# Sums of squares of queries and keys: one fp32 product or two fp32r products of split squares

## The chip, the cores and the metric

The kernel runs on one core of one Trainium2 chip. The metric is the device time of one execution in microseconds (us), the median of several runs. A core has TensorE (PE, which multiplies matrices, its weight loads are written PEld), VectorE (DVE), ScalarE (ACT), GpSimd (POOL), and SyncE (SP), whose queue issues most of the DMAs.

## What is computed

One step of a two-layer streaming encoder for 1024 frames of a new stream and 32 frames of a running one, 1056 tokens in all, model width 1024. Layer 0 mixes tokens by forgetting attention with 16 heads of 64 features, layer 1 by a gated linear recurrence; each is followed by a squared-ReLU MLP. The change touches the norms of queries and keys in layer 0, one norm for each token and head:

```python
def rmsnorm(x, g):
    xf = x.astype(jnp.float32)
    y = xf * lax.rsqrt(jnp.mean(xf * xf, axis=-1, keepdims=True) + EPS)
    return (y * g.astype(jnp.float32)).astype(x.dtype)

def fox_mixer(h, w_in, b_f, g_q, g_k, w_out, past_k, past_v, past_logf):
    proj = h @ w_in
    q = proj[..., :D_MODEL].reshape(B, T, FOX_HEADS, FOX_HEAD_DIM)
    k = proj[..., D_MODEL:2 * D_MODEL].reshape(B, T, FOX_HEADS, FOX_HEAD_DIM)
    ...
    q = rmsnorm(q, g_q)
    k = rmsnorm(k, g_k)
```

## The kernel before

Everything is fp32 in and out. The large products run in fp32r, a form of fp32 with fewer bits: each operand is split into a high part (the value rounded to fp32r) and a low part (what is left), and a product is three fp32r products (`mm3`, L152 to L158, all recorded at L158). A weight is split in `load_w` (L122 to L146): rounded on ScalarE or GpSimd, subtracted on VectorE.

The 1056 tokens are three chunks of 352 columns (`C`), with features on the 128 partitions. In `fox`, pairs of heads (128 features) are taken one after the other. For a pair, `fox_pair` makes the projections v, k and q, three chunks each, 24 products a chunk (`proj`, tile `pj`); `fox_attend` then does the attention of the pair in two halves: first the row maxima of the logits (`mp`, reduced on VectorE), then, block by block, logits (`st`), their exponentials on ScalarE (`pf`), the split of these on GpSimd (`ph`, after a causal mask on the diagonal blocks) and VectorE (`pl`), and the products with the values (`pv`). The next pair's projections run beside the attention of the pair before: v and k mostly beside the maxima, q beside the second half.

Each chunk of k and of q goes through `ev_norm` (L745 to L757). ScalarE copies the product out of PSUM (`raw`, L750) and squares it (`sq`, L751). TensorE sums the squares over the 64 features of each head, and spreads the sum over these 64 partitions, by a product with `blk`, a matrix of two blocks of ones (`ss`, L753, fp32). `rsqrt` (L197 to L210) takes that to the power -1/2: a logarithm and an exponential on ScalarE (L203, L206), a Newton step of three instructions on VectorE (L208 to L210, with a scratch tile of tag `nt`). L756 multiplies. There are 8 pairs x 2 x 3 = 48 such chunks.

Buffers on this path: `pj` and `ss` share two PSUM buffers (tag A), `raw` and `sq` have two buffers each, `nt` and `qr` one each. Raw weights have two buffers (tag `wr`).

`late_consts` (L94 to L97) loads `blk` and the causal mask `tri` with one DMA while the first chunk is normed. It is called behind the first weight loads.

The order of instructions on each engine is not the order of the text. The framework plans it when the kernel is built, by the priority of an instruction (its place in the text, unless raised) and by when its inputs and a buffer for its output are expected to be ready. At run time each engine goes through its own list in order and waits on semaphores.

Of the kernel before, what the change touches and what calls it, by code (L numbers as in the profile page):

```python
# [7 lines left out]
F32 = mybir.dt.float32  # L8
F32R = mybir.dt.float32r
# [24 lines left out]
def consts():  # L34
# [11 lines left out]
    # pairs of key s and query t: in one block of four, then in the two halves of larger blocks  # L46
# [13 lines left out]
class K:  # L60
# [21 lines left out]
    def gains(self):  # L82
        # gains, features of a tile on partitions: loaded in rows, turned on the tensor engine
# [9 lines left out]
    # constants that the first products do not need  # L93
    def late_consts(self):  # L94
        m = self.cp.tile([128, 2, 128], F32, name="mats")
        self.nc.sync.dma_start(m, self.io["c_mats"][:, 1:3])
        self.blk, self.tri = m[:, 0], m[:, 1]  # L97
# [7 lines left out]
    # what frees PSUM goes ahead of other work  # L105
# [3 lines left out]
    # an order of two instructions on one engine  # L109
# [11 lines left out]
    # one unit of weights: [128, X, Y] with X*Y = 1024, split exactly into two float32r parts  # L121
# [29 lines left out]
    # out += W^T x over the given k tiles; each product in three float32r passes  # L151
# [12 lines left out]
    # per token of a chunk, tokens on partitions in three columns (the last one overlaps the  # L164
    # second): sums over all features of s, [128, C]
# [8 lines left out]
    # such columns as rows along the free axis, the same on every partition  # L174
# [7 lines left out]
    # running sum over feature tiles of y ** 2: [128, C], features of a tile on partitions  # L182
# [13 lines left out]
    # r = (ss / n + eps) ** -0.5  # L196
    def rsqrt(self, r, ss, n, pool):  # L197
# [9 lines left out]
        # one Newton step  # L207
# [13 lines left out]
    # x * gain in split form; y is scratch  # L221
# [13 lines left out]
    # the norm's factor per token, which the products take on later: as columns, or as rows  # L235
    def prestat(self, x, y, rows):
# [13 lines left out]
        # the product's factor is the square, which the norm after it takes to the square again  # L250
# [4 lines left out]
    # the norm's factor per token of y * sc, for y; ss the sums of y ** 2  # L255
# [14 lines left out]
    # x += rmsnorm(y * sc), sc a factor per token, acc the sum of y ** 2; y is overwritten  # L270
# [52 lines left out]
    # the last chunk of the output is normed with tokens on partitions, in three blocks (the last  # L323
    # one overlaps the second). Ahead of that: x in that form, and the gains on diagonals
# [43 lines left out]
    # one token chunk of the input: loaded with tokens on partitions,  # L368
# [11 lines left out]
    # brought to features on partitions, with the first norm's factor per token,  # L380
# [37 lines left out]
    # normed and split  # L418
# [14 lines left out]
    # mixer's output (features on partitions, split, per token chunk) -> W_out -> norms ->  # L433
    # squared-ReLU MLP -> norms; returns the next layer's h, or writes the outputs
    def tail(self, os, w_out, layer, rs=None, after=None):
# [5 lines left out]
        with ExitStack() as c:  # L441
# [10 lines left out]
            # output projection  # L452
# [3 lines left out]
            # a factor of the norm before the products is less urgent than the next chunk's norms  # L456
# [24 lines left out]
            # MLP, G tiles of the hidden layer at a time  # L481
# [27 lines left out]
            # one output tile of the second matrix, over the given hidden tiles  # L509
# [27 lines left out]
            # the first three tiles of the hidden layer token chunk by token chunk, as the norms finish  # L537
# [12 lines left out]
            for g in range(NG - 2):  # L550
# [8 lines left out]
                for o in range(NJ):  # L559
                    for n in range(NCH):  # L560
                        down_one(g == 0, us, dw, o, n)
                us = nxt
            # the last two groups token chunk by token chunk, so that the norms overlap the products;
            # the last group's second weights in an h tile that is free by then
            dw = down_w(NG - 2)
            w = up_w(NG - 1)
            nxt = [u_tile() for i in range(G)]
# [751 lines left out]
```

## Time and profile before

| what | value |
|---|---|
| time, median of 3 runs | 2999.41 us (2998.34 to 3000.39) |
| span of the profiled execution | 2996.0 us |
| TensorE busy | 2942.2 us, 98% |
| VectorE busy | 1734.0 us, 58% |
| ScalarE busy | 934.1 us, 31% |
| GpSimd busy | 967.0 us, 32% |

The profile is one execution of the program. Its span lies 3.4 us under the median of the runs. PE's busy time includes the time in which one matmul fills the array while the one before drains, so a busy PE is not one at its peak. Register, semaphore and DMA-issuing instructions are not counted as busy. The forgetting attention's part lies in the first 700 us.

### The profile page before, as it was taken

To read this page: it belongs to the slowest core of one execution; us is meant where nothing else is said; L and a number is where in the kernel's file an instruction comes from. 1 tells how busy PE (TensorE), PEld (TensorE's weight loads), DVE (VectorE), ACT (ScalarE), POOL (GpSimd) and SP (SyncE) were. 2 spreads that over 40 slices of the span, in tenths; PEclk is the share of its full clock that TensorE was granted. 3 is DMA by queue.
4 is the path that set the end of the run, shared out by engine and by line. 5 is a ranking of instruction groups with operands and counts; after the bars stand their busy time and mean duration, and the time that the engine had idled before them with its cause. 6 is when DMAs were issued, how large, how long until landed. Compare 5 with 4: busy or idle time off the path is not lost.

```text
span 2996.0 us, 46448 instructions
## 1 busy us (share of the span) xinstructions
PE 2942.2 (98%) x18511; PEld 2855.2 (95%) x18511; DVE 1734.0 (58%) x2980; ACT 934.1 (31%) x1915; POOL 967.0 (32%) x1151
## 2 busy tenths in 40 slices
PE   7999999999999999999998999999999999999999
PEld 6888888899999999999997999999999999999998
DVE  6788888874544444445468656654474454454545
ACT  5455555555432111111133122212353111111112
POOL 3345444531432112121145444433362121121223
PEclk9999999999999999999999999999999999999999
DMA  5221121134321111121122111104432111111112
GB/s 152 62 52 44 48 53 48 51 112 147 106 74 57 43 43 50 36 57 49 37 82 95 35 59 41 47 27 120 140 118 76 36 57 43 43 50 36 57 61 69
DMA packets 217817, 195.59 MB, mean 65 GB/s; under 512 B 14312, under 2 KB 193648, under 8 KB 217472
## 3 DMA queue, kind: packets, MB, share of 16 engines
q1 hardware_dynamic: 216576, 192.49, 21.5%
q8 instruction: 145, 2.38, 0.3%
q14 instruction: 72, 0.59, 0.1%
q0 software_dynamic: 1024, 0.13, 0.0%
HBM read 147.00 MB, written 45.52 MB: 64 GB/s over the span
## 4 chain that ended last, share of the span: by engine, by line
PE 89%; DVE 5%; issue 1%; POOL 1%; ACT 1%; DMA 1%; SPq 0%; DVEq 0%; POOLq 0%; ACTq 0%
PE up L158 24%; PE dn L158 24%; PE hj L158 8%; PE pj L158 8%; PE gp L158 6%; PE po L158 5%; PE lv L1166 1%; PE ss L753 1%; PE pv L880 1%; PE pv L879 1%; PE pv L878 1%; PE st L867 1%; PE st L866 1%; PE mp L835 1%; PE lv L1181 1%
## 5 line engine op out<-in xcount | busy, mean ns | idle before, releaser
L520 DVE TENSOR_TENSOR ya<-dn,ya 128x352 f32<-128x352 f32 x672 | 348.3, 522 | 550.4 <-PE dn L158 550.4
L162 POOL TENSOR_TENSOR rl<-rl 128x352 f32<-128x352 f32 x192 | 190.2, 999 | 1031.7 <-ACT uh L501 1029.3
L145 DVE TENSOR_TENSOR wl<-wr,wh 128x1024 fp32r<-128x1024 f32 x203 | 280.4, 1382 | 147.0 <-ACT wh L142 84.6
L158 PE MATMUL dn<-uh,wl 128*128 128x352 f32 x1440 | 356.9, 323 | 0.0
L158 PE MATMUL dn<-uh,wh 128*128 128x352 f32 x1440 | 353.7, 324 | 2.5 <-DVE ya L520 2.5
L158 PE MATMUL dn<-ul,wh 128*128 128x352 f32 x1440 | 353.5, 323 | 0.0
L499 ACT ACTIVATE rl<-up 128x352 f32<-128x352 f32 x192 | 88.8, 463 | 783.1 <-PE up L158 712.8
L158 PE MATMUL up<-hh,wl 128*128 128x352 f32 x1536 | 291.5, 323 | 0.0
L158 PE MATMUL up<-hh,wh 128*128 128x352 f32 x1536 | 287.5, 323 | 2.1 <-ACT wh L142 1.7
L158 PE MATMUL up<-hl,wh 128*128 128x352 f32 x1536 | 288.1, 323 | 0.0
L158 PEld LDWEIGHTS up<-hh,wh 128*128 128x128 f32 x1536 | 253.5, 188 | 3.1 <-ACT wh L142 2.3
L158 PEld LDWEIGHTS dn<-uh,wh 128*128 128x128 f32 x1440 | 251.3, 188 | 4.4 <-DVE ya L520 4.4
L158 PEld LDWEIGHTS up<-hh,wl 128*128 128x128 f32 x1536 | 254.4, 188 | 0.0
L158 PEld LDWEIGHTS up<-hl,wh 128*128 128x128 f32 x1536 | 254.1, 188 | 0.0
L158 PEld LDWEIGHTS dn<-uh,wl 128*128 128x128 f32 x1440 | 252.6, 188 | 0.0
L158 PEld LDWEIGHTS dn<-ul,wh 128*128 128x128 f32 x1440 | 251.8, 188 | 0.0
L144 POOL TENSOR_SCALAR wh<-wr 128x1024 fp32r<-128x1024 f32 x109 | 120.8, 1108 | 294.3 <-PE pj L158 93.0
L503 DVE TENSOR_TENSOR ul<-rl,uh 128x352 fp32r<-128x352 f32 x192 | 142.6, 754 | 124.9 <-POOL rl L162 124.8
L142 ACT CAST wh<-wr 128x1024 fp32r<-128x1024 f32 x94 | 98.7, 1050 | 347.2 <-PE up L158 221.5
L876 DVE TENSOR_TENSOR pl<-pf,ph 128x512 fp32r<-128x512 f32 x192 | 124.5, 652 | 59.9 <-POOL ph L875 34.7
L875 POOL TENSOR_SCALAR ph<-pf 128x512 fp32r<-128x512 f32 x192 | 125.2, 654 | 51.6 <-PE pv L879 24.7
L869 ACT ACTIVATE pf<-st,ncol 128x512 f32<-128x512 f32 x192 | 109.7, 578 | 71.2 <-PE st L867 40.1
(343 smaller groups left out, 5673.0 us busy)
## 6 DMA issues: line engine op xcount, KB each, us to landing
wr<-in_ffn_w_up_dram SPq DMA_DIRECT2D x64, 512.0 KB, 4.0
wr<-in_ffn_w_down_dram SPq DMA_DIRECT2D x64, 512.0 KB, 3.8
wr<-in_fox_w_in_dram SPq DMA_DIRECT2D x32, 512.0 KB, 4.1
wr<-in_hgrn_w_in_dram SPq DMA_DIRECT2D x32, 512.0 KB, 4.1
x<-xd SPq DMA_DIRECT2D x22, 704.0 KB, 4.9
xd<-x SPq DMA_DIRECT2D x18, 704.0 KB, 3.1
out_dram<-tk SPq DMA_DIRECT2D x32, 256.0 KB, 2.4
odg<-go SPq DMA_DIRECT2D x30, 176.0 KB, 2.5
```

The lines of the kernel that those rows point to most:

```text
L142: self.s.copy(wh, raw)
L144: self.g.tensor_scalar(out=wh, in0=raw, scalar1=1.0, scalar2=0.0, op0=ALU.mult, op1=ALU.add)
L145: self.v.tensor_tensor(wl, raw, wh.bitcast(F32), op=ALU.subtract)
L158: self.nc.tensor.matmul(ps, lhsT=ws[kk][a], rhs=xs[kk][b], start=i == 0, stop=i == tot - 1)
L162: self.g.tensor_tensor(out, a, b, op=op)
L499: self.s.activation(rl, ps[:, :C], AF.Relu)
L503: self.v.tensor_tensor(ul, rl, uh.bitcast(F32), op=ALU.subtract)
L520: self.v.tensor_tensor(ys[n][:, o], ps[:, :C], ys[n][:, o], op=ALU.add)
L753: nc.tensor.matmul(ss[:, :C], lhsT=self.blk, rhs=sq, start=True, stop=True)
L869: self.s.activation(pf[:, :N], ps[:, :N], AF.Exp, bias=self.ncol[:, b, head:head + 1])
L875: self.g.tensor_scalar(out=ph[:, :N], in0=pf[:, :N], scalar1=1.0, scalar2=0.0, op0=ALU.mult, op1=ALU.add)
L876: self.v.tensor_tensor(pl[:, :N], pf[:, :N], ph[:, :N].bitcast(F32), op=ALU.subtract)
```

## The change

The square of a chunk is split in two fp32r parts, as weights are: ScalarE rounds it (`sh`), GpSimd subtracts (`sl_`), and the fp32 product with `blk` becomes two fp32r products that add up in PSUM. `sh` takes the second buffer of tag `sq`, `sl_` the single buffer of tag `nt`. `blk` is made fp32r by a copy on VectorE, from a raw tile of tag `wr`; its load and that of `tri` are two DMAs. Comments are removed all over the file, so most line numbers stay. The lines that count:

```diff
     def late_consts(self):
-        m = self.cp.tile([128, 2, 128], F32, name="mats")
-        self.nc.sync.dma_start(m, self.io["c_mats"][:, 1:3])
-        self.blk, self.tri = m[:, 0], m[:, 1]
+        self.tri = self.cp.tile([128, 128], F32, name="tri")
+        self.nc.sync.dma_start(self.tri, self.io["c_mats"][:, 2])
+        m = self.wp.tile([128, 128], F32, name="bl", tag="wr", bufs=2)
+        self.nc.sync.dma_start(m, self.io["c_mats"][:, 1])
+        self.blk = self.cp.tile([128, 128], F32R, name="blk")
+        self.v.tensor_copy(self.blk, m)
...
                 self.s.copy(raw, ps)
                 self.s.activation(sq, ps, AF.Square)
+                sh = pool.tile([128, C], F32R, name=f"sh{u}", tag="sq", bufs=2)
+                sl_ = pool.tile([128, C], F32R, name=f"sl{u}", tag="nt", bufs=1)
+                self.s.copy(sh, sq)
+                self.gtt(sl_, sq, sh.bitcast(F32), ALU.subtract)
                 ss = psp.tile([128, 512], F32, name=f"ss{u}", tag="A", bufs=2)
-                nc.tensor.matmul(ss[:, :C], lhsT=self.blk, rhs=sq, start=True, stop=True)
+                nc.tensor.matmul(ss[:, :C], lhsT=self.blk, rhs=sh, start=True, stop=False)
+                nc.tensor.matmul(ss[:, :C], lhsT=self.blk, rhs=sl_, start=False, stop=True)
```

## Rows read from the trace of the kernel before

**Rows 1.** The page: span, busy time and share of each engine, instructions.

```profile
span 2996.0 us, 46448 instructions
...
PE 2942.2 (98%) x18511; PEld 2855.2 (95%) x18511; DVE 1734.0 (58%) x2980; ACT 934.1 (31%) x1915; POOL 967.0 (32%) x1151
```

**Rows 2.** The page: the chain that ended last, by engine.

```profile
PE 89%; DVE 5%; issue 1%; POOL 1%; ACT 1%; DMA 1%; SPq 0%; DVEq 0%; POOLq 0%; ACTq 0%
```

**Rows 3.** Table by stage: length, busy us (instructions) of each engine, clock, DMA.

```profile
80.00:90.00 10.00, 7.34 (x38) 6.04 (x37) 9.81 (x15) 4.95 (x9) 4.66 (x5) 0.83 0.31 81
90.00:100.00 10.00, 9.06 (x55) 8.05 (x54) 6.91 (x15) 4.96 (x11) 1.03 (x1) 1.00 0.20 56
...
130.00:590.00 460.00, 454.65 (x2594) 409.04 (x2594) 382.94 (x810) 249.34 (x500) 221.03 (x369) 1.00 0.19 48
```

**Rows 4.** Groups to 1100 us: out<-in, shape, count | busy us, mean ns | idle before.

```profile
L158 PE MATMUL pj<-hl,wh 128*128 128x352 f32 x576 | 127.2, 327 | 0.0
...
L753 PE MATMUL ss<-sq,mats 128*128 128x352 f32 x96 | 39.9, 498 | 7.2 <-ACT sq L751 7.1
...
L426 ACT CAST hh<-y 128x352 fp32r<-128x352 f32 x24 | 11.5, 485 | 13.2 <-DVE y L424 13.0
```

**Rows 5.** Timeline beside the attention's second half: start us, us, instruction, count [wait].

```profile
136.73 0.76 PE L753 MATMUL ss<-sq,mats 128*128 128x352 f32 x2
137.06 1.72 PE L158 MATMUL pj<-hh,wh 128*128 128x352 f32 x8
138.62 1.45 PE L158 MATMUL pj<-hh,wl 128*128 128x352 f32 x8
...
157.27 0.47 ACT L751 ACTIVATE sq<-pj 128x352 f32<-128x352 f32 x1
...
159.72 0.75 PE L753 MATMUL ss<-sq,mats 128*128 128x352 f32 x2
```

**Rows 6.** Tile hl to 130 us: count, ns min/median/max, first and last start.

```profile
L430 DVE TENSOR_TENSOR hl<-y,hh x18: 509/517/2675, 19.7 to 66.4; 128x352 fp32r<-128x352 f32 x18
L162 POOL TENSOR_TENSOR hl<-y,hh x6: 942/1068/1205, 19.2 to 62.2; 128x352 fp32r<-128x352 f32 x6
```

**Rows 7.** Timeline beside the maxima, a chunk of k of pair 1.

```profile
121.83 0.79 PE L835 MATMUL mp<-KB,QX 96*128 96x512 f32 x3
...
122.35 0.47 ACT L751 ACTIVATE sq<-pj 128x352 f32<-128x352 f32 x1
...
122.87 0.86 PE L753 MATMUL ss<-sq,mats 128*128 128x352 f32 x2 [0.26 <-ACT sq L751]
...
123.30 1.72 PE L158 MATMUL pj<-hh,wh 128*128 128x352 f32 x8
...
124.89 0.53 DVE L208 SCALAR_TENSOR_TENSOR nt<-ss,qr 128x352 f32<-128x352 f32 x1 [0.74 <-ACT qr L206]
```

**Rows 8.** Timeline of pair 0, first chunk of q.

```profile
84.66 1.54 PE L753 MATMUL ss<-sq,mats 128*128 128x352 f32 x2 [1.31 <-ACT sq L751]
...
85.48 2.78 PE L158 MATMUL pj<-hh,wh 128*128 128x352 f32 x8
```

**Rows 9.** Waits to 620 us: who <- whom, us in total, times, longest.

```profile
PE ss L753 <- ACT sq L751: 7.1, 21, 1.3
...
PE pv L878 <- POOL ph L875: 1.3, 4, 0.3
```

**Rows 10.** Timeline of SP's queue and of GpSimd at the start.

```profile
11.57 0.42 SPq L132 DMA_DIRECT2D wr<-in_fox_w_in_dram  x1
12.05 0.57 SPq L96 DMA_DIRECT2D mats<-in_c_mats_dram  x1
...
17.86 2.26 SPq L631 DMA_DIRECT2D xd<-x  x4
...
21.52 2.50 POOL L139 TENSOR_TENSOR wl<-wr,wh 128x1024 fp32r<-128x1024 f32 x1
```

**Rows 11.** Tile ss, product with blk: records, ns min/median/max, first and last start.

```profile
L753 PE MATMUL ss<-sq,mats x96: 457/459/956, 39.7 to 587.0; 128*128 128x352 f32 x96
```

## The prediction

> **What bounds the kernel now.** I read the page first: TensorE is busy for 98% of the span, no other engine for more than 58% [rows 1], and the chain that ended last lies on PE for 89% of it [rows 2]. So time on PE is time of the kernel, unless PE is waiting. The change touches only the forgetting attention, so the second view is the table of stages. From 130 to 590 us, where pairs 1 to 7 are projected beside the attention of the pair ahead, PE is busy for 454.65 of 460 us at the full granted clock (1.00, that is 2.4 GHz); VectorE for 383, ScalarE for 249, GpSimd for 221 [rows 3]. Ahead of that, with pair 0 alone, PE has 0.9 to 2.7 us of idle time in ten, and in one stretch the granted clock is 0.83 [rows 3].
>
> Third view: the groups. The product with blk runs 48 times (8 pairs, q and k, 3 chunks) and shows as 96 records, two for each fp32 product [rows 4]. What one holds of PE is read from its neighbours: `ss` starts at 136.73, the eight `pj` behind it take 1.72 us where the next eight take 1.45 [rows 5], so the first of them was held back by 0.27 us and starts in effect at 137.32. One `ss` holds PE for 0.59 us. Eight `pj` of fp32r in 1.45 us, one of them lasting 0.33 (the mean of `pj`), are (1.45 - 0.33)/7 = 0.16 us each [rows 4, 5].
>
> **The change, part by part.** *The product in two passes.* Two fp32r products of the same 352 columns take 2 x 0.16 = 0.33 us in place of 0.59: 0.26 us less on PE for each, 48 x 0.26 = 12.5 us in all. In the saturated stretch and just ahead of it lie the 42 of pairs 1 to 7: 42 x 0.26 = 11. The six of pair 0 lie where PE waits anyway; I count nothing for them.
>
> The Trainium skill (Trainium Kernel Development and Optimization, Performance Expectations) holds matmul busy time a bad measure, because matmuls are pipelined, and takes the busy share of LDWEIGHTS. Here the two differ, 454.65 against 409.04 us of 460 [rows 3]; by that rule only 89% of the stretch is filled, and the 11 us would be 9.8.
>
> *Removed wait, added wait.* Today `ss` needs the square. From now on it needs the square, a copy of it to fp32r on ScalarE and the subtraction on GpSimd. The copy: 0.49 us, as the cast of a tile of this size from SBUF [rows 4]. The subtraction: 1.07 us, between 0.94 and 1.21, as the one `hl` of this shape on GpSimd [rows 6]. Hop between engines 0.05 us (square ends at 122.82, `ss` starts at 122.87 [rows 7]). So the sums start 1.65 us later; the product itself ends 0.49 us after its start and no longer 0.76 [rows 5], so the factor is 1.4 us later.
>
> Who waits for that? Queued behind `ss` on PE is the next chunk of the projection, 24 products or 3.9 us. It shares two PSUM buffers with `ss`: one is held by the chunk just done until its square is read, the other goes to `ss`. In 46 of the 48 the next product of a projection or gate stands directly behind `ss` (three of them are in [rows 5, 7, 8]; behind the first two come the forget gates'); both come free with the square. With the change the chunk is ready 1.6 us before `ss`, and since the order on each engine is planned ahead by readiness and priority, I take it that the 24 products go first and `ss` falls among them. Then the chunk covers the new wait. Beside the attention's second half there is more cover: at 157.27 the square begins, `ss` stands at 159.72 only, because attention's products rank ahead [rows 5]: the 1.6 us fit into that 2 us.
>
> What does not fit: in the first half (the maxima, `mp`), three short products fill the gap, then PE waits 0.26 us for the square [rows 7]; 21 such waits are 7.1 us in all [rows 9]. If `pj` takes the place of `ss` there, it waits for the same square, so that stays; if the free buffer lets it start at once, the waits vanish. Bounds: 0 to -7 us; I take 0, nearest to the rows.
>
> Lateness: PE goes in its fixed order, so a subtraction that comes later than planned holds up everything behind `ss`. The nearest row is the attention's own chain over the same engines, `st`, ScalarE, GpSimd, `pv`: in 192 of them PE waits four times, 1.3 us in all, 0.3 at most [rows 9]. Bounds: 0 to 48 x 0.3 = 14 us; I take 1, by that row.
>
> *Load on the other engines.* ScalarE gets 48 x 0.49 = 24 us, GpSimd 48 x 1.07 = 51 us; in the stretch they go from 54% to 59% and from 48% to 58%, no bound. VectorE gains no instruction but company: the same subtraction on VectorE ranges from 0.51 to 2.68 us in the first 130 us [rows 6], and I put the spread down to GpSimd's work beside it. If each of the 42 costs VectorE between 0 and 1.07 us, that is up to 45 of its 77 idle us; PE waits for it rarely. I take 1 us.
>
> *Buffers.* sh is the second `sq` buffer, free once the `ss` before it is done. sl is the one `nt` buffer, which the Newton step of the chunk before holds. That loop: subtraction 1.07, from `ss` to the first Newton step 2.0 us (122.87 to 124.89), three steps of 0.53 [rows 7]: 4.7 us against 3.9 + 0.33 = 4.2 us of PE per chunk when nothing lies between, as in pair 0, and about 6 beside `mp`. So at most 0.5 us for a few chunks of pair 0. There the chain from the square to the next chunk is on the path (1.31 us of wait at 84.66, and the next eight `pj` take 2.78 us, at about half the clock, after that idle time [rows 8]); bounds for the four late chunks: 4 x 1.4 = +5.6 if nothing covers, -2 if the wait goes. I take +1.
>
> *Constants.* One DMA of two matrices becomes two, and blk's half goes through a weight buffer (`wr`) and a copy on VectorE. On SP's queue it stands behind the weight load at 11.57; waiting for a buffer, it can hold back the stores of x and the small loads behind it until GpSimd has split those weights, at 24.0 [rows 10]. blk is first used at 39.7 [rows 11]. The copy is under the 0.51 us of a tile 2.75 times as wide. Cover 15 us: nothing; were it gone, the loads of the third chunk's x would come later, some 3 us.
>
> **The sum.** -11 + 0 + 1 + 1 + 1 = -8, rounded outward a little for the waits that may go: -9. The profiled span is 2996.0 us [rows 1], so 2987 by the profile; the median of the runs is 3.4 us above that span, which the change leaves as it is: 2990.4, say 2990. About 0.2% (6 us) is what a measurement of this kernel can tell from no change; 9 us is 0.3%.
>
> **The rivals.**
> *More than the passes.* The next `pj` uses the free PSUM buffer at once, and PE no longer empties at each `ss` beside `mp` and in pair 0: 7 us of waits [rows 9] and some of the emptied pipeline go too. 2990 - 11 = 2979. For it: PE did nothing else in the gaps; against: in today's order no `pj` stands ahead of the `ss` before it.
> *Given back.* `ss` is planned too early, the subtraction stands in GpSimd's queue behind ph, or ph behind it, and PE waits 0.26 us each: the gain of the passes is gone, 2999. For it: PE already waits 7.1/21 = 0.34 us at an `ss` for a chain of two steps that was planned to be ready [rows 9]; against: `pv` [rows 9].
> *PE waits out the subtraction.* If the next `pj` may not take its PSUM buffer before `ss` has one, PE has nothing but `mp` in the new 1.4 us. Place: the 21 `ss` of k in pairs 1 to 7 and six of pair 0. Price 27 x 1.4 - 12.5 = +25 us, 3024. It decides from the point where the mean new wait at an `ss` is above 0.26 us. For it: `ss` ahead of `pj` without exception; against: both come free with the same square, which explains that too. The Trainium skill (GPSIMD Engine Reference, 4.1 Engine selection) speaks against the place of the subtraction: it puts a two-input elementwise operation on GpSimd at about twice VectorE's time and sends it to VectorE; the trace agrees, 1068 against 517 ns [rows 6], and what hangs on it is the longest link of the new wait.
> *The passes are no shorter.* If fp32r products on blk took as long as the halves of the fp32 one, 0.3 us, nothing is gained: 3001. Against it speak all `pj`.
>
> **How the numbers follow.** Forecast 0.50, more than the passes 0.12, given back 0.18, waits out 0.17, no shorter 0.03. The forecast's own range, 2985 to 2997, has some 0.04 of its 0.50 within 0.2%; given back has 0.03 of its 0.18 beyond 0.2% on the slow side. Faster 0.46 + 0.12 = 0.58; same 0.04 + 0.15 + 0.03 (no shorter) = 0.22; slower 0.17 + 0.03 = 0.20. The range goes from 2976 to 3012: the low end takes in the first rival and its bound, the high end the bound of lateness (14 us) and half of the way into the third rival; what is left out is under 0.2.
>
> **What would show it.** `ss` as 96 fp32r records of about 0.32 us, 0.33 us from the first to the next `pj`; `ss` standing among `pj` of the next chunk; the group of waits of PE at `ss` for GpSimd small (under 3 us); the stage from 130 to about 590 shorter by 8 to 11 us, and everything behind it unchanged but earlier. Wrong would be: PE waiting for `sl` at most `ss`, `pj` still directly behind `ss`, or longer waits at `pv` for ph.

## The result, and the profile of the changed kernel

The changed kernel takes 3041.9 us in the median (3038.6 to 3042.9), the kernel before 2999.4: 42.5 us or 1.4% slower, ratio 1.0137 [1.0125, 1.0149]. The forecast was 2990, and its range ended at 3012.

Where the time went is read in three steps. First the page of the changed kernel: its span is 45.2 us longer, and the busy time of TensorE (PE) has not become less, as the shorter passes would have it, but 13.5 us more than in [rows 1].

```profile
span 3041.2 us, 46598 instructions
...
PE 2955.7 (97%) x18511; PEld 2867.5 (94%) x18511; DVE 1751.6 (58%) x2981; ACT 946.9 (31%) x1963; POOL 1036.1 (34%) x1199
```

Second, a landmark behind the change: the first product of the MLP, `up`. It starts at 817.9 us in the kernel before and at 861.6 in the changed one; the last starts at 2938.7 and 2984.0. So 43.7 of the 45 us are lost ahead of the MLP, in the forgetting attention. (Columns: instructions, ns min/median/max, first and last start. Kernel before, then the changed kernel.)

```profile
L158 PE MATMUL up<-hh,wh x1536: 317/323/430, 817.9 to 2938.7; 128*128 128x352 f32 x192
```

```profile
L161 PE MATMUL up<-hh,wh x1536: 317/323/427, 861.6 to 2984.0; 128*128 128x352 f32 x192
```

Third, the table by stage (columns as in [rows 3]). The first `ss` of pair 1 starts at 116.8 us in the kernel before and at 130.0 in the changed one, so nearly equal work lies from 30 to those points (458 and 446 of PE's records), and from there to the first `up`. The kernel before:

```profile
30.00:116.80 86.80, 77.51 (x458) 69.93 (x456) 61.86 (x130) 43.41 (x101) 23.64 (x23) 0.98 0.35 99
116.80:817.90 701.10, 692.64 (x4037) 638.41 (x4038) 534.01 (x1094) 372.56 (x748) 305.61 (x487) 1.00 0.26 72
```

The changed kernel, with the stretch of [rows 3] beside it:

```profile
30.00:130.00 100.00, 80.36 (x446) 73.29 (x444) 61.87 (x126) 44.58 (x104) 31.64 (x29) 0.91 0.30 87
130.00:861.60 731.60, 700.91 (x4040) 645.42 (x4040) 551.58 (x1100) 382.74 (x789) 368.41 (x529) 0.98 0.24 69
...
130.00:590.00 460.00, 434.35 (x2444) 389.82 (x2444) 374.27 (x783) 239.21 (x500) 255.59 (x371) 0.98 0.17 45
```

Pair 0 costs 13.2 us more (100.0 against 86.8), the rest of the attention 30.5 (731.6 against 701.1). PE's idle time (length less busy time) grows from 9.3 to 19.6 us in the first part and from 8.5 to 30.7 in the second, 32.6 us together. Its busy time grows by 2.9 and 8.3 us. The passes took 12.5 us off it, so some 24 us of busy time are work at a lower clock: the granted clock is 0.91 and 0.98 in place of 0.98 and 1.00 (an estimate from these rows). From 130 to 590 us PE idles 25.7 us, against 5.4 in [rows 3].

The passes are as short as forecast: 0.33 us each where [rows 11] had two records of 0.46.

```profile
L761 PE MATMUL ss<-sh,blk x48: 318/326/662, 37.8 to 637.0; 128*128 128x352 f32 x48
...
L762 PE MATMUL ss<-sl,blk x48: 318/327/432, 38.6 to 641.3; 128*128 128x352 f32 x48
```

The waits of PE up to 620 us, to be held against [rows 9]. The subtraction (L165, sl) is near the end of the list, 0.9 us in all. In front stand other works of ScalarE and VectorE, none of which the change touches: tk, pl, the casts hh, the maxima mx. Beside them PE waits 2.2 us, in three, for a Newton step (nt) that had yet to read `ss` and so to free its PSUM buffer.

```profile
PE to L776 <- ACT tk L778: 8.8, 7, 2.7
PE pv L889 <- DVE pl L885: 6.7, 10, 1.4
PE fz L161 <- ACT hh L429: 6.6, 7, 3.1
PE st L875 <- DVE mx L852: 5.0, 4, 1.3
...
PE ss L762 <- POOL sl L165: 0.9, 2, 0.6
```

What has happened is in the timeline of a chunk of k, pair 1, beside the maxima as in [rows 7] (start us, us, instruction, [idle before it <- releaser]). TensorE:

```profile
130.00 0.42 PE L761 MATMUL ss<-sh,blk 128*128 128x352 f32 x1
130.25 1.46 PE L161 MATMUL pj<-hh,wh 128*128 128x352 f32 x8
...
134.12 0.32 PE L762 MATMUL ss<-sl,blk 128*128 128x352 f32 x1
...
136.71 0.43 PE L761 MATMUL ss<-sh,blk 128*128 128x352 f32 x1
...
142.03 0.33 PE L762 MATMUL ss<-sl,blk 128*128 128x352 f32 x1
...
145.75 0.47 PE L875 MATMUL st<-QA,KA 128*128 128x512 f32 x1 [1.26 <-DVE mx L852]
...
146.72 2.58 PE L161 MATMUL pj<-hh,wh 128*128 128x352 f32 x8
```

GpSimd and ScalarE in the same stretch:

```profile
130.01 0.96 POOL L165 TENSOR_TENSOR sl<-sq,sh 128x352 fp32r<-128x352 f32 x1 [4.70 <-ACT sh L758]
...
139.37 1.36 POOL L165 TENSOR_TENSOR sl<-sq,sh 128x352 fp32r<-128x352 f32 x1 [1.38 <-DVE qr L213]
...
134.48 0.55 ACT L206 ACTIVATE qr<-ss,eps 128x352 f32<-128x352 f32 x1 [4.54 <-PE ss L762]
...
136.17 0.48 ACT L758 CAST sh<-sq 128x352 fp32r<-128x352 f32 x1
```

The two passes of a chunk no longer stand together. The high pass goes at 130.00, right behind the copy. The subtraction ends at 130.97, yet the low pass goes only at 134.12, behind 21 of the next chunk's 24 products, because that is its place in PE's order. ScalarE sat idle for 4.54 us until it could take the logarithm of the factor. The next chunk's high part is ready at 136.65, but its subtraction starts at 139.37: it writes the one `nt` buffer, which the late Newton step before it (qr L213) still holds. Its low pass stands at 142.03. At 144.49 the next product in PE's order is an `st` that waits for a row maximum; PE idles 1.26 us, and the next eight `pj` take 2.58 us where the eight at 130.25 took 1.46.

A late factor can be followed from its low pass to a wait of PE in pair 0. The subtraction ends at 84.55; the low pass stands at 86.31, behind 21 `pj`, and ScalarE is idle for 5.59 us until it can take the logarithm. Exponential, Newton step and kh follow; kh ends at 90.74. ScalarE's copies of kh (KA, 2.11 us) then stand ahead of the copy tk, and the next transposition on PE (`to`) waits 2.65 us for that copy.

```profile
86.31 0.32 PE L762 MATMUL ss<-sl,blk 128*128 128x352 f32 x1
86.67 0.55 ACT L206 ACTIVATE qr<-ss,eps 128x352 f32<-128x352 f32 x1 [5.59 <-PE ss L762]
90.16 0.58 DVE L765 SCALAR_TENSOR_TENSOR kh<-raw,gq,qr 128x352 f32<-128x352 f32 x1
91.12 2.11 ACT L815 CAST KA<-kh 64x1024 fp32r<-64x1024 f32 x2
93.25 0.58 ACT L778 COPY tk<-to 128x512 f32<-128x512 f32 x1
93.89 0.39 PE L776 MATMUL to<-ident,vT 128*32 128x128 f32 x1 [2.65 <-ACT tk L778]
```

In PE's order of instructions the last pass over a chunk's squares stands on the mean 40 products behind the chunk's own last product; in the kernel before it was 8.

### The profile page after: what moved, and what is told of

The parts are those of the page before. It is cut to its first block, busy times and chain, and to the rows that moved or that the text cites. A ratio compares the mean times of both kernels' runs of the same rounds, so it can differ in the third digit from the quotient of the medians.

```text
span 3041.2 us, 46598 instructions
## 1 busy us (share of the span) xinstructions
PE 2955.7 (97%) x18511; PEld 2867.5 (94%) x18511; DVE 1751.6 (58%) x2981; ACT 946.9 (31%) x1963; POOL 1036.1 (34%) x1199
## 4 chain that ended last, share of the span: by engine, by line
PE 86%; DVE 8%; issue 2%; DMA 2%; ACT 1%; POOL 1%; SPq 0%; DVEq 0%; POOLq 0%; ACTq 0%
PE dn L161 24%; PE up L161 23%; PE hj L161 9%; PE pj L161 7%; PE gp L161 6%; PE po L161 5%; PE lv L1175 1%; PE st L875 1%; PE st L876 1%; PE pv L889 1%; PE pv L888 1%; PE pv L887 1%; PE mp L844 1%; DVE hl L234 1%; DVE mx L849 1%
## 5 line engine op out<-in xcount | busy, mean ns | idle before, releaser
L165 POOL TENSOR_TENSOR rl<-rl 128x352 f32<-128x352 f32 x192 | 188.4, 989 | 1033.2 <-ACT uh L504 1031.0
L884 POOL TENSOR_SCALAR ph<-pf 128x512 fp32r<-128x512 f32 x192 | 132.8, 697 | 33.1 <-ACT pf L878 10.4
```

The source lines that it names most:

```text
L165: self.g.tensor_tensor(out, a, b, op=op)
L884: self.g.tensor_scalar(out=ph[:, :N], in0=pf[:, :N], scalar1=1.0, scalar2=0.0, op0=ALU.mult, op1=ALU.add)
```

## The experiments

The theory that I started from (A) was that the split of the group costs the time: one pass early, which takes the PSUM buffer, and one late. The rivals: the `nt` buffer shared with the Newton step (B), and the load of the added instructions themselves (C). The order on each engine is planned anew for every kernel, so an edit changes more than its own lines. PE's products ahead of the first `up`, `ss` aside, stand in one and the same order in the kernel before and in the constants alone, in the passes alone and the run with half the weight, and in the two runs with the passes together; in no other two kernels here do they. All ratios are to the kernel before on the same chip, which took 2998.5 to 3000.7 us there. Diffs are against the changed kernel unless another is named. "Behind" is the place of the last pass, in products behind its own chunk.

| kernel | behind | median us | ratio | first `up`, us |
|---|---|---|---|---|
| before | 8 | 2999.4 | 1 | 817.9 |
| changed | 40 | 3041.9 | 1.0137 [1.0125, 1.0149] | 861.6 |
| constants alone | 8 | 3002.6 | 1.0004 [0.9995, 1.0014] | 818.9 |
| passes alone | 9 | 2988.8 | 0.9960 [0.9945, 0.9975] | 806.8 |
| + unread copy | 8 | 3008.0 | 1.0029 [1.0016, 1.0042] | 823.9 |
| + copy, read | 13 | 3008.4 | 1.0025 [1.0016, 1.0035] | 828.0 |
| + unread subtraction, VectorE | 13 | 3011.8 | 1.0044 [1.0027, 1.0061] | 830.1 |
| + unread subtraction, GpSimd | 12 | 3021.1 | 1.0071 [1.0056, 1.0086] | 839.6 |
| the same, second pass late | 34 | 3061.7 | 1.0200 [1.0186, 1.0214] | 875.7 |
| changed, passes together | 17 | 3081.0 | 1.0273 [1.0258, 1.0288] | 900.1 |

### Passes together, own buffer, and both

Three runs set A against B. Together:

```diff
-matmul(ss[:, :C], lhsT=self.blk, rhs=sh, start=True, stop=False)
-matmul(ss[:, :C], lhsT=self.blk, rhs=sl_, start=False, stop=True)
+matmul(ss[:, :C], lhsT=self.blk, rhs=sl_, start=True, stop=False)
+matmul(ss[:, :C], lhsT=self.blk, rhs=sh, start=False, stop=True)
```

> The two passes swap: the low part opens the group of `ss`, the high part closes it, so that nothing of the group can start before the subtraction is done, and both passes stand next to each other. In the order of TensorE's instructions the last pass now stands 17 products behind its own chunk on the mean, against 40 in the changed kernel and 8 in the kernel before; buffers, engines and counts stay. Theory A (the group is pulled apart: its high pass takes the PSUM buffer at once, the low pass is ordered behind the next chunk, and the factor, the copies of queries and keys and the first product of the chunk after that come late): most of the 42 us comes back, 2995 to 3015. Theory B (the subtraction shares the one nt buffer with the Newton step before it): nothing comes back, 3030 to 3045. Theory C (the added work itself loads ScalarE, GpSimd and VectorE too much): nothing comes back, 3035 to 3045.

Own buffer for the low part:

```diff
-sl_ = pool.tile([128, C], F32R, name=f"sl{u}", tag="nt", bufs=1)
+sl_ = pool.tile([128, C], F32R, name=f"sl{u}", tag="sl", bufs=1)
...
-tag="qk", bufs=2
+tag="qk", bufs=1
...
-tag="mr", bufs=2
+tag="mr", bufs=1
```

> The low part has a buffer of its own in place of the nt one, paid for with one buffer less of each of two small tiles (mr and qk); the passes stay apart. The last pass stands 34 products behind its own chunk in TensorE's order. Theory A: little comes back, as 34 is near 40: 3025 to 3042. Theory B: the loop through the Newton step is cut, 2995 to 3010. Theory C: 3035 to 3045.

Both edits:

> Both edits at once: low part first and in a buffer of its own (mr and qk one buffer less). The last pass stands 17 products behind its chunk, as with the swap alone. Theory A: as the swap alone, within 4 us: 2993 to 3013. Theory B: as the own buffer alone, 2995 to 3010. Theory C: 3035 to 3045.

Measured: together 3081.0, own buffer 3036.5, 1.0123 [1.0108, 1.0138], both 3081.0, 1.0271 [1.0254, 1.0289]. The runs with the passes together lie above the ranges of all three theories. Theory A as I had it falls: with the group in one piece and its last pass at 17 products the kernel is 39 us slower still. B as I priced it (2995 to 3010) falls as well: with its own buffer the kernel takes 5 us less (the intervals of 1.0123 and 1.0137 overlap), and none less where the passes stand together. What the two small tiles lose by their one buffer less isn't shown. The own buffer's 3036.5 lies in the ranges of A and of C.

The trace of the first shows the third rival of the prediction, "PE waits out the subtraction", at work. PE's waits from 30 to 680 us:

```profile
PE pv L889 <- DVE pl L885: 24.5, 16, 3.1
PE ss L761 <- POOL sl L165: 19.0, 16, 4.8
```

They are of two kinds. In eight of the 16 waits (10.9 us) GpSimd was free and began sl within 0.14 us of the end of sh: there PE waits out the chain of copy and subtraction, up to 3.2 us at a time. In the other eight (8.1 us) sl stood in GpSimd's order behind other work. The longest is of this kind, in pair 0: ahead of sl stands the split of a weight unit (wh), which waited 3.34 us for its DMA. The high part had been ready at 84.19 (ScalarE, the cast at 83.71). And behind the wait the next 16 `pj` take 2.55 and 2.40 us in place of twice 1.46.

```profile
83.71 0.48 ACT L758 CAST sh<-sq 128x352 fp32r<-128x352 f32 x1
...
84.14 2.62 POOL L147 TENSOR_SCALAR wh<-wr 128x1024 fp32r<-128x1024 f32 x1 [3.34 <-DMA wr<-in_fox_w_in_dram]
86.72 0.92 POOL L165 TENSOR_TENSOR sl<-sq,sh 128x352 fp32r<-128x352 f32 x1
...
87.70 0.66 PE L761 MATMUL ss<-sl,blk 128*128 128x352 f32 x1 [4.78 <-POOL sl L165]
...
88.45 2.55 PE L161 MATMUL pj<-hh,wh 128*128 128x352 f32 x8
90.80 2.40 PE L161 MATMUL pj<-hh,wl 128*128 128x352 f32 x8
```

So with the group split PE waits 0.9 us for sl, and with the passes together 19.0; the price of the split is the late factor.

### The subtraction made and not read

```diff
-matmul(ss[:, :C], lhsT=self.blk, rhs=sl_, start=False, stop=True)
+matmul(ss[:, :C], lhsT=self.blk, rhs=sh, start=False, stop=True)
```

> Copy and subtraction are made as in the changed kernel, in the same buffers, but the second pass reads the high part once more and not the low one, so that no product waits for the subtraction (the sums of squares are then those of twice the high part). Instructions and their counts on each engine are those of the changed kernel; the last pass stands 12 products behind its chunk. Theory A: the gain that was forecast from the shorter passes shows, 2985 to 3000. Theory B: the subtraction still shares nt with the Newton step and holds the next Newton step up a little, 2990 to 3010. Theory C: the load is the same as in the changed kernel, so 3030 to 3045.

Measured 3021.1, 1.0071. It lies between the bounds of the theories: 20 us of the loss go with the dependence, but 21 us stay although nothing waits for the subtraction. So the loss has parts, and the next four runs take the change apart from the other end. New theories: the copy lengthens the chain to the first pass (D), the added instructions load their engines (E), the constants delay the start (F). From here on, runs whose passes read one part twice leave out the low part and add up twice the squares; they are for their time alone.

### The change, one part after the other

Constants alone:

```diff
-self.blk = self.cp.tile([128, 128], F32R, name="blk")
+self.blk = self.cp.tile([128, 128], F32, name="blk")
...
-self.s.copy(sh, sq)
-self.gtt(sl_, sq, sh.bitcast(F32), ALU.subtract)
...
-matmul(ss[:, :C], lhsT=self.blk, rhs=sh, start=True, stop=False)
-matmul(ss[:, :C], lhsT=self.blk, rhs=sl_, start=False, stop=True)
+matmul(ss[:, :C], lhsT=self.blk, rhs=sq, start=True, stop=True)
```

> Of the change only the two separate loads of the constants at the start stay (tri and blk by themselves, blk copied by VectorE, here as float32); squares and passes are those of the kernel before. Theory D (the chain from a chunk's last product to its first and last pass of `ss` has grown longer) and theory E (the added instructions load the engines beside TensorE): nothing, 2994 to 3003. Theory F (the constants delay the start, seen as the 12 us by which the pair 0 of the changed kernel ends later): 3008 to 3014.

Measured 3002.6, 1.0004: nothing, F falls.

Passes alone:

```diff
-sq = pool.tile([128, C], F32, name=f"sq{u}", tag="sq", bufs=2)
+sq = pool.tile([128, C], F32R, name=f"sq{u}", tag="sq", bufs=2)
...
-self.s.copy(sh, sq)
-self.gtt(sl_, sq, sh.bitcast(F32), ALU.subtract)
...
-matmul(ss[:, :C], lhsT=self.blk, rhs=sh, start=True, stop=False)
-matmul(ss[:, :C], lhsT=self.blk, rhs=sl_, start=False, stop=True)
+matmul(ss[:, :C], lhsT=self.blk, rhs=sq, start=True, stop=False)
+matmul(ss[:, :C], lhsT=self.blk, rhs=sq, start=False, stop=True)
```

> ScalarE writes the squares as float32r at once; no copy, no subtraction; TensorE makes two float32r passes over that one part (the sums are then those of twice the rounded squares). Chain length and engine load are those of the kernel before, only the passes are shorter. If the forecast priced the passes rightly (48 times 0.26 us, less what was given back), 2985 to 2993; if time saved in a pass is waited out somewhere else, 2995 to 3001. Theories D and E agree here; F adds 12 us to either.

Measured 2988.8, 0.9960: 12 us faster, the 11 that the forecast had for the passes. In the table by stage, from 130 to 590 us, the clock stays at 1.00 and PE idles 7.4 us:

```profile
130.00:590.00 460.00, 452.57 (x2657) 416.65 (x2656) 388.40 (x828) 256.41 (x512) 232.77 (x376) 1.00 0.19 51
```

Copy without subtraction:

```diff
-self.gtt(sl_, sq, sh.bitcast(F32), ALU.subtract)
...
-matmul(ss[:, :C], lhsT=self.blk, rhs=sl_, start=False, stop=True)
+matmul(ss[:, :C], lhsT=self.blk, rhs=sh, start=False, stop=True)
```

> As the run with the unread subtraction (3021), but without the subtraction: ScalarE copies the squares to a float32r high part and both passes read it (sums of twice the high part). Theory D: the copy is in the chain, so nearly all of the 22 us stays: 3010 to 3022. Theory E (GpSimd's subtraction is the load that hurts, also when nobody reads it): 2985 to 2997. In between, 2997 to 3010, both share it.

Measured 3008.4, 1.0025. The copy costs 20 us over the passes alone (1.0025 less 0.9960), the unread subtraction another 14 (1.0071 less 1.0025), its being read another 20 (1.0137 less 1.0071). With the -12 of the passes that makes up the +42; each difference of two ratios is uncertain by some 5 us. These steps are differences between kernels that were planned separately: the price of a part and that of the new order around it come together in each of them.

The subtraction on VectorE:

```diff
-self.gtt(sl_, sq, sh.bitcast(F32), ALU.subtract)
+self.v.tensor_tensor(sl_, sq, sh.bitcast(F32), op=ALU.subtract)
```

> The subtraction moves from GpSimd to VectorE, all else as in the changed kernel: same buffer nt, low pass apart from the high one (43 products behind its own chunk in TensorE's order, 40 in the changed kernel). Theory D: a subtraction that takes 0.5 us and not 1.0 us shortens the real chain but not the order: 3030 to 3045. Theory E with GpSimd as the loaded engine: 3000 to 3020. If VectorE, 83 to 86 percent busy in these stages, is the engine that is late next: 3045 to 3070.

Measured 3049.6, 1.0161 [1.0146, 1.0176]: no better, rather 7 us worse, though the subtraction now takes 0.52 us in the median, not 1.24. It is in the range expected for VectorE as the engine that is late next (3045 to 3070). The low pass stands 43 products behind here, so a shorter subtraction did not bring it forward; which of the two costs the 7 us isn't shown. The Trainium skill (GPSIMD Engine Reference, 4.1 Engine selection) would have such an operation on VectorE; here the durations agree with it and the kernel's time does not.

### Why parts that nobody waits for cost time

The copy made and not read (against the run with the passes alone), and the same with a buffer of its own (tag sh, one buffer; mr and qk one less):

```diff
+sh = pool.tile([128, C], F32R, name=f"sh{u}", tag="sq", bufs=2)
+self.s.copy(sh, sq.bitcast(F32))
 matmul(ss[:, :C], lhsT=self.blk, rhs=sq, start=True, stop=False)
```

> The run with the passes alone (2989), plus the copy of the squares on ScalarE into the second sq buffer, which nobody reads (the passes read the squares as they are). ScalarE's instructions and buffers are those of the run with the copy read (3008). Theory D (the copy costs because the passes wait for it): 2987 to 2994. Theory E (the copy costs because it takes ScalarE 0.5 us and a buffer, whoever reads it): 3003 to 3010. In between, both share the 20 us.

> The run with the unread copy (3008), the copy now in a buffer of its own, so that the two sq buffers serve two chunks again (mr and qk one buffer less). If the copy cost through the sq buffer: 2987 to 2995. If it costs as ScalarE's time or through the order: 3002 to 3012.

Measured 3008.0 and 3005.9, 1.0021 [1.0011, 1.0031]. So the copy costs the same read and unread, and the second `sq` buffer isn't the reason: theory D falls. What a copy can do at the start is seen on ScalarE. In the kernel before the next chunk's first hh cast goes ahead of the logarithm of the factor (57.01, then 57.52). In the run with the unread copy the order has become sh, logarithm, exponential, and only then the hh casts; PE sat idle 1.55 us for the first of them. ScalarE's timeline of the kernel before, then ScalarE and PE in the run with the unread copy:

```profile
57.01 0.49 ACT L426 CAST hh<-y 128x352 fp32r<-128x352 f32 x1 [0.44 <-DVE y L424]
57.52 0.56 ACT L203 ACTIVATE qr<-ss,eps 128x352 f32<-128x352 f32 x1
```

```profile
60.30 0.49 ACT L757 CAST sh<-sq 128x352 fp32r<-128x352 f32 x1
60.90 0.56 ACT L206 ACTIVATE qr<-ss,eps 128x352 f32<-128x352 f32 x1
...
61.89 1.63 ACT L429 CAST hh<-y 128x352 fp32r<-128x352 f32 x4
...
62.41 0.43 PE L161 MATMUL fz<-hh,wh 128*128 128x352 f32 x1 [1.55 <-ACT hh L429]
```

This run's first transposed k comes 6 us later than in the run with the passes alone (104.1 against 98.3 us). Waits of PE for hh make up 3.5 of them (5.7 us up to 70 us, against 2.2): the 1.55 shown, and a longer one of 2.62 at 48.87, just ahead of which ScalarE has no sh but another instruction that waited for VectorE. In the run with the copy's own buffer that part is gone (98.7), and the total is the same; there the time is lost in the pairs behind. Why the sum stays at 17 to 20 us I could not settle; ScalarE's time and the new order come together in both runs.

The unread subtraction on VectorE (against the run with it on GpSimd):

```diff
-self.gtt(sl_, sq, sh.bitcast(F32), ALU.subtract)
+self.v.tensor_tensor(sl_, sq, sh.bitcast(F32), op=ALU.subtract)
```

> The run with the unread subtraction (3021; GpSimd sat 41 us before it, waiting for the copy), with the subtraction on VectorE in place of GpSimd. If the 13 us over the run without a subtraction (3008) came from GpSimd being held up, in its order, by an instruction that waits: 3006 to 3013. If any unread subtraction costs this (its buffers, the nt tile it shares): 3017 to 3024. If VectorE is the tighter engine: 3024 to 3040.

Measured 3011.8, 1.0044, against 3021.1 on GpSimd and 3008.4 with none. So 8 or 9 of the 14 us go when the subtraction leaves GpSimd, although that engine is busy for little more than half of the stretch (254.6 of 460 us). The trace of the run on GpSimd shows two things. GpSimd is held, in its order, for the copy (its waits from 130 to 620 us):

```profile
POOL sl L165 <- ACT sh L758: 46.0, 12, 6.7
```

And VectorE's subtraction pl of the attention takes longer, 107.7 us in all against 98.1 in the run without a subtraction; PE's waits at `pv` for it are 5.2 us from 130 to 620, against 2.6. Nearly all of the increase lies with one of its four shapes, 128x256; 128x512 grows a little, and the other two hardly change. (Groups by shape from 130 to 550 us, columns as in [rows 4]; first the run without a subtraction.)

```profile
L883 DVE TENSOR_TENSOR pl<-pf,ph 128x512 fp32r<-128x512 f32 x72 | 58.7, 828 | 13.2 <-POOL ph L882 10.8 <-ACT sq L754 1.6 <-PE pv L887 0.7
L883 DVE TENSOR_TENSOR pl<-pf,ph 128x256 fp32r<-128x256 f32 x24 | 11.4, 474 | 3.8 <-POOL ph L882 3.6
```

```profile
L885 DVE TENSOR_TENSOR pl<-pf,ph 128x512 fp32r<-128x512 f32 x72 | 61.6, 866 | 10.9 <-POOL ph L884 9.4 <-ACT pf L878 1.6
L885 DVE TENSOR_TENSOR pl<-pf,ph 128x256 fp32r<-128x256 f32 x24 | 19.4, 808 | 3.3 <-POOL ph L884 3.2
```

In the longer 128x256 instructions GpSimd works beside pl for 0.72 of 0.81 us, 0.19 of it on sl; in the shorter ones for 0.30 of 0.47. The Trainium skill (GPSIMD Engine Reference, 1. Specifications) says that GpSimd shares its way into SBUF with VectorE and that VectorE's instructions with two inputs from SBUF contend with it; pl is such an instruction, and the 128x256 shape agrees. How these 8 or 9 us split between the two causes and the new order no run tells.

The late second pass, without a subtraction to wait for (against the run with the unread subtraction on GpSimd):

```diff
-nc.tensor.matmul(ss[:, :C], lhsT=self.blk, rhs=sh, start=False, stop=True)
...
+def second():
+    p2 = nc.tensor.matmul(ss[:, :C], lhsT=self.blk, rhs=sh, start=False, stop=True)
+    self.behind(p2, self.last_mm)
...
+pend.append(second)
```

(`last_mm` is the last product so far; `second` runs behind the products of the next chunk, with the factor in it.)

> The run with the unread subtraction (3021), whose second pass reads the high part again, with that second pass held behind the last product of the next chunk (for two of three chunks of a projection; the third has none behind it). The last pass then stands 34 products behind its chunk on the mean (12 in the run with the unread subtraction, 40 in the changed kernel) and nothing waits for the subtraction. The sums are twice those of the high part. If the late place of the second pass is what costs the 20 us: 3033 to 3045. If the subtraction's own lateness costs them: 3015 to 3027.

Measured 3061.7, 1.0200: 39 us over the same kernel with its second pass in place (1.0200 less 1.0071), beyond the 12 to 24 expected. No instruction was added; one product of 0.33 us and the factor behind it were moved, and the order around them was planned anew. So a late second pass, with the order that comes with it, can cost as much as the changed kernel's last 20 us and more, although PE doesn't wait at these passes; it waits at `pv` (waits up to 620 us), and the clock falls (table by stage):

```profile
PE pv L901 <- DVE pl L897: 16.6, 9, 3.0
```

```profile
130.00:590.00 460.00, 429.55 (x2366) 382.38 (x2366) 363.76 (x750) 236.26 (x492) 239.60 (x368) 0.96 0.17 44
```

Five of the nine waits at `pv` are of 2.96 or 2.97 us, one in each of five pairs, and each time VectorE's order is the same: the split of a weight unit (wl) and the low part of k (KA) stand ahead of the pl for which `pv` waits.

```profile
254.86 2.87 DVE L148 TENSOR_TENSOR wl<-wr,wh 128x1024 fp32r<-128x1024 f32 x1
257.75 1.22 DVE L828 TENSOR_TENSOR KA<-kh,KA 64x1024 fp32r<-64x1024 f32 x1
259.00 0.69 DVE L897 TENSOR_TENSOR pl<-pf,ph 128x512 fp32r<-128x512 f32 x1
...
259.75 0.50 PE L901 MATMUL pv<-pl,VH 128*128 128x512 f32 x1 [2.96 <-DVE pl L897]
```

VectorE works through these without a gap. KA needs the factor, the weight split does not. So the 39 us are not lateness by itself, and that the 20 us of the changed kernel are lateness and nothing besides isn't shown; its passes stand at other places than here.

### How far order alone moves the time

One pass (against the run with the passes alone):

```diff
-matmul(ss[:, :C], lhsT=self.blk, rhs=sq, start=True, stop=False)
-matmul(ss[:, :C], lhsT=self.blk, rhs=sq, start=False, stop=True)
+matmul(ss[:, :C], lhsT=self.blk, rhs=sq, start=True, stop=True)
```

> The low part is left out: ScalarE writes the squares as float32r at once and TensorE makes a single pass over them (the squares are rounded to float32r before they are added up). No copy, no subtraction, no second pass. The run with two passes over them took 2989; one pass less is 48 times 0.16 us off TensorE: 2978 to 2985 if all of it shows, 2985 to 2990 if it is waited out.

Measured 3000.2, 1.0002 [0.9992, 1.0011]: 12 us slower than with two passes, with less work, and 20 us above what its work alone (8 us less) would make it. Squares twice (with a buffer of its own for the low part, as above):

```diff
-self.s.copy(raw, ps)
-self.s.activation(sq, ps, AF.Square)
...
-self.s.copy(sh, sq)
+self.s.activation(sh, ps, AF.Square)
+self.s.activation(sq, ps, AF.Square)
+self.s.copy(raw, ps)
```

> All of the change's arithmetic with a shorter chain: ScalarE squares the chunk twice out of PSUM, first to the float32r high part, then to float32, and copies raw last; there is no copy of the squares, and the low part has a buffer of its own (mr and qk one buffer less). The first pass stands 9 products behind its chunk, the last 23 (12 and 40 in the changed kernel). If the length of the chain up to the last pass is what costs, the time falls between the unread subtraction (3021) and the shorter passes alone: 3000 to 3020, and it would beat the kernel before only under 2994. If the split of the group costs whatever its distance: 3025 to 3040.

Measured 3023.3, 1.0082 [1.0067, 1.0097]: with the last pass at 23 products, 16 us of the 42 come back, between the two ranges expected; up to 5 of them may be the own buffer's. Swap of two ScalarE instructions, in the kernel before, in the run with the passes alone and in that with one pass:

```diff
-self.s.copy(raw, ps)
 self.s.activation(sq, ps, AF.Square)
+self.s.copy(raw, ps)
```

> The kernel before with two ScalarE instructions swapped: the square of a chunk first, the copy to raw behind it. No instruction is added or taken away; `ss` stands 7 products behind its chunk in TensorE's order, 8 in the kernel before. If the time hangs on work and chain length alone: 2994 to 3000 (the square is done 0.5 us earlier, and TensorE waited 7 us in all for it). If the order that the planner makes of it moves the time by itself: anything from 2985 to 3015, outside 2994 to 3000.

> The run with the passes alone (2989) with the same swap of the square and the copy to raw. If the 12 us are the passes' own: 2984 to 2990, 12 us under the run with only the swap. If the order moves the time as much as the passes do: up to 3005, and the difference to the run with only the swap is not 12.

> One pass over squares rounded to float32r (3000 without the swap; the low part is left out), with the swap of the square and the copy to raw. By work alone 8 us under the run with two passes and the same swap: 2976 to 2985. If order decides: 2985 to 3005.

Measured: in the kernel before 2999.2, 0.9996 [0.9987, 1.0005]; with two passes 2994.7, 0.9981 [0.9971, 0.9990]; with one pass 2995.1, 0.9986 [0.9976, 0.9995]. The swap changes the kernel before by nothing, makes the run with two passes 6 us slower and the one with one pass 5 us faster. With the swap two passes gain 6 us, not the 12.5 of their work, and one pass gains 4, not 20 (12.5 and 48 times 0.16). So the swap moves the time by some 5 us either way once anything else is changed, and the run with one pass lies 16 to 20 us above its work. Of the 12 us that the work of the two passes promises, 6 to 12 show. The steps of 14 and 20 us above are no larger than what the order did here, so how much of each belongs to its part and how much to the new order stays open.

Two passes with half the weight (against the run with the passes alone):

```diff
-self.v.tensor_copy(self.blk, m)
+self.v.tensor_scalar(out=self.blk, in0=m, scalar1=0.5, scalar2=None, op0=ALU.mult)
```

> The run with the passes alone (2989) with the constant blk halved, so that the two passes over the squares rounded to float32r give the sums themselves (the low part is left out, as in the run with one pass). Instructions and order are those of the run with the passes alone: 2986 to 2992, ratio to the kernel before 0.995 to 0.9975, if that run's time is the order's and comes back; 2995 to 3003 if it was an accident of the run.

Measured 2991.2, 0.9967 [0.9955, 0.9979]. It beats both kernels, with the sums taken over squares rounded to float32r, that is without the low part; its first `up`, at 806.7 us, stands where it stood in the run with the passes alone. So the time of one order comes back.

## Why the prediction was wrong

**What bounds the kernel** was read rightly: 43.7 of the 45 us that were lost are PE idle or PE at a lower clock, ahead of the first `up`.

**The passes: right.** 0.33 us in place of 0.59 as 96 records; alone they gain 12 us, in another order 6, forecast 11; the run with one pass, which should have gained 20, gained 0 to 4. **The constants: right**, 1.0004. That blk's DMA might hold up the start did not happen; the first `ss` even starts 1.9 us earlier.

**The step that failed** is "I take it that the 24 products go first and `ss` falls among them. Then the chunk covers the new wait." The observation came true, for the low pass, and so did the small waits: 0.9 us at sl, under the 3 us that were to confirm the forecast. The conclusion did not. I asked only whether PE would wait at `ss`, and took the factor to be 1.4 us late. It is late by the whole place in the order: 3.15 us from the end of the subtraction to the low pass in the stretch shown, and 40 products behind the chunk in place of 8. Who waits for the factor was not followed: ScalarE's logarithm, the next subtraction, the copies of q and k, and through ScalarE's order tk and `to`, as in the chain from 86.31 to 93.89. How far the waits for `mx` and `pl` come from the factor was not traced. The step from an unread to a read subtraction costs 20 us, a late second pass with its new order 39; the forecast had 0 + 1.

**Load on the other engines** was the second failure, and by size the larger, 34 of the 54 us that the passes' gain had to cover. "No bound" was read off busy shares of a long stretch, 54 and 48%. The unread copy costs 20 us and the unread subtraction 14, each with the order planned around it; the forecast had 0 and 1. The spread of hl in [rows 6] from 0.51 to 2.68 us was a hint for VectorE: pl took 9.6 us more beside the unread subtraction. I took 1 from "PE waits for it rarely"; PE's waits at `pv` for pl doubled from 2.6 to 5.2 us.

**Pair 0** was priced at +1, with a bound of 5.6, and cost 13.2. I counted the chain of four late chunks. In the changed kernel the largest new waits of PE there are for tk, 5.1 us in four and none before, then for hh (3.5 us against 1.7) and for the Newton step that frees the buffer of `ss` (1.8 us); PE's clock is 0.91 in place of 0.98.

**The `nt` loop** I put at half a microsecond for a few chunks of pair 0. In the trace it is plain (2.7 us at 139.37), but with it cut the kernel takes only 5 us less, which the intervals don't tell from none.

**The rivals.** "PE waits out the subtraction" had the right sign; its place and its price did not fit. In the changed kernel PE waits there for 0.9 us in all. Where it does wait, with the passes together, the waits are 19.0 us in 16, up to 4.8 each and not 1.4, and the kernel is 82 us slower than before, not 25. Of the 19.0, 10.9 are the chain of copy and subtraction, as this rival had it, and 8.1 are GpSimd's queue, as "given back" had it. No rival had the case that came: hardly a wait at the changed instruction, and the loss at others.

**The tests named in the prediction** did not cut. Three of the four were met or nearly met by a kernel that is 42 us slower; only the fourth, the stage from 130 to 590 us, was not.

## What to carry to other kernels

Where the bounding engine is 98% busy in an order that was planned for it, an added step on a half-idle engine can cost time even where nothing waits for its result: ask of each added instruction not only who waits for it, but where its consumer is put in the order and who needs that consumer's result. A product group fed by two engines at different times may be pulled apart by a planner; look at the place of its last member before pricing its wait. And price a gain of 0.4% in such a kernel against what reordering alone moves: here some 5 us by the swap of two instructions, and 16 to 20 us in the runs with one pass.

## What the runs showed of the hardware

Two things that I had not expected. An idle time of PE can be paid twice: after 1.26 us the eight `pj` at 146.72 took 2.58 us, at a granted clock of 0.52 (close to the lower level, 1.2 GHz); after 4.78 us eight took 2.55 and the next eight 2.40, at 0.50 and 0.53; at the full clock eight take 1.46. It is not so each time: after 1.27 us at the same place of another pair the eight `pj` at 298.77 took 1.54. In the changed kernel as a whole an estimated 24 us of lower clock stand beside 33 us of new idle time. And GpSimd's order can count for more than its load: in the run with the passes together, where it is busy for 31 of the 100 us from 30 to 130, it held sl for 2.5 us behind a weight split that waited for its DMA.
